# Attention's output projection as four pairs of column tiles by seven block products

## The chip, the core and the metric

The kernel runs on one core of one Trainium2 chip. The metric is the device time of one execution in microseconds (us); three runs gave 1574.85, 1574.91 and 1575.28, median 1574.91.

## What is computed

One inference step of a one-layer streaming encoder, width 1024, on 512 prompt frames and 64 sample frames (576 columns in all, held transposed: features on partitions, frames as columns), in float32:

```python
h = layer_norm(ALPHA * x + 0.5 * swiglu_ffn(x, w_gu, w_down))
z = h @ w_in        # mLSTM q, k, v, o, i, f | attention q, k, v | gates g_ml, g_att
o = band_attention(qa, ka, va)
y_att = o.reshape(b, t, ATT_WIDTH) @ p['w_att_proj']
merged = jax.nn.sigmoid(g_ml) * y_ml + jax.nn.sigmoid(g_att) * y_att
h = layer_norm(ALPHA * h + merged @ p['w_out'])
y = layer_norm(ALPHA * h + 0.5 * swiglu_ffn(h, w_gu2, w_down2))
```

The change is in `y_att`, a product of 1024 by 1024 weights and 1024 by 576 attention outputs, which is then multiplied by the sigmoid of the attention gates.

## The kernel before, in words

**Products.** Every float32 operand is kept as a hi part (rounded, `fp32r`) and a lo part (the rest). A product is three matmuls: hi by hi, hi by lo, lo by hi (`mm3`, and the loops in `gemm` and `product`); `wh`, `wl` are the parts of weights, `os` those of the attention output, `H` those of the layer's input. A column tile is 128 output features; its weights are 1024 columns of SBUF (eight blocks of 128 by 128).

**Plain stages.** `gemm` takes column tiles one after the other, each in two halves of the frames (256 and 320 columns), 24 matmuls a half. Weights come in the order of the list `plan`: `pump` loads a tile on the SP queue into `wr` (two buffers), ScalarE makes the hi part, and for tiles in `ADDED` the lo part comes from ScalarE (minus the hi part) and a second, adding load that GpSimd issues (`add_lo`); other tiles' lo parts are made by VectorE. Four pairs of `wh`, `wl` are there (`NWB`). `pump` converts no tile past the index `wst["stop"]`, which comes from the list `stops`.

**Units by seven products.** In both feed-forwards and in part of the input projection, two column tiles by the two halves of the frames (288 columns each) are made as a unit: with the weights in four blocks and the input in four blocks, seven products of sums of blocks take the place of eight (class `Units`; `Columns` for the input projection). A product is four 128-row blocks by three matmuls, 12 matmuls of 288 columns, and a unit is 84. `Combos.add` makes the sums of the input's blocks, `prep` those of the weights and their parts (`a`: the raw blocks `a12`, `a11`; `s`: sums; `t`, `u`, `b`: parts of sums and of `a22`), by ScalarE (hi) and VectorE (lo, sums). `run` writes out the order: `a11` by `b11`, `a12` by `b21`, in the first unit also the next one's `a11`; then `s2` by `t2`, `s1` by `t1`, `s3` by `t3`, and, after the next unit's first product, `a22` by `t4` and `s4` by `b22`.

**The stage around the change.** After attention's eight pairs of heads, six column tiles of attention's gates (columns 64 to 69 of `w_in`) are plain `gemm`s; gates 6 and 7 were made earlier and lie in DRAM (`GD`). Inside the fourth of them (`j == 3`) attention's pools are closed and the background job `os_split` starts: it splits the eight tiles of attention output (`OT`) into `os` and applies the sigmoid to the first four gates. Background jobs and `later` calls are written into the program while matmuls are counted (`od.tick`). The projection follows: eight plain tiles `("ap", j)`, all in `ADDED`; `ap_cb` multiplies the gate tile by each half on VectorE and stores it to DRAM (`MD`). Behind it starts the mLSTM, with column tiles 8, 9, 0, 1 of `w_in` and their convolution.

TensorE's order is as written; on the other engines and the DMA queues a scheduler orders the instructions by the program and priorities.

Of the kernel before, what the change touches and what calls it, by code (L numbers as in the profile page):

```python
# [10 lines left out]
F32 = mybir.dt.float32  # L11
F32R = mybir.dt.float32r
# [5 lines left out]
P = 128  # L18
# [63 lines left out]
def tile_layer(ctx: ExitStack, tc: tile.TileContext, ins, outs):  # L82
# [30 lines left out]
    def away(s):  # L113

        return dram.tile([P, T], F32, name=nm(s))
# [25 lines left out]
    def act(out, in_, func=AF.Copy, **kw):  # L141
        return ACT.activation(out, in_, func, **kw)  # L142

    def tt(out, a, b, op, eng=None):
        return (eng or DVE).tensor_tensor(out, a, b, op=op)  # L145
# [12 lines left out]
    def blank(out, like, behind=None):  # L158
# [229 lines left out]
    def one(key):  # L388
        return [[(key, KT)]]
# [587 lines left out]
    class Columns(Units):  # L977
# [19 lines left out]

        def done(self, u):
            self.sinks[u["j"]](u["o"])

    class Hidden(Act):

# [620 lines left out]

        act(hs(sg[j], hf), ps, AF.Copy if j <= 3 else AF.Sigmoid)

    for j in range(KT):
        s = slot(F32)
        sg.append(s)
        if j > 5:
            SP.dma_start(s, GD[j])  # L1630
            continue
        gemm(one(("in", 64 + j)), H, [lambda hf, ps, j=j: keep_cb(hf, ps, j)])
        if j == 3:
            od.drain()
            astack.close()
            od.force(lambda: gdone)
            tstack.close()
            ospool = tc.tile_pool(name="os", bufs=16, reuse_waits="tile")
            osp = ostack.enter_context(ospool)
            OS = Act()  # L1640

            osq = []

            def os_split():
                for o_ in OT:
                    hi, lo = slot(F32R, osp, "os"), slot(F32R, osp, "os")
                    act(hi, o_)
                    tt(lo, o_, f(hi), ALU.subtract)
                    yield None
                    OS.p.append((hi, lo))  # L1650
# [7 lines left out]
    MD = [away("md") for _ in range(KT)]  # L1658

    def ap_cb(j):  # L1660
        def cb(hf, ps):
            m = hs(sg[j], hf)
            tt(m, m, ps, ALU.mult)
            if hf == 1:
                SP.dma_start(MD[j], sg[j])
                sg[j] = None
        return cb

    for j in range(KT):
        gemm(one(("ap", j)), OS, [ap_cb(j)])  # L1670
    ostack.close()


# [452 lines left out]
```

## Time and profile before

| what | value |
|---|---|
| runs | 1574.85, 1574.91, 1575.28 us (median 1574.91) |
| profiled execution, its span | 1571.7 us (its own run time is not given apart; the median of the runs lies 3.2 above) |
| TensorE, VectorE, ScalarE, GpSimd busy | 1548.6, 1082.4, 895.5, 214.4 us |
| the projection on TensorE | 801.12 to 852.31 us, no idle time |
| gate tiles 4 and 5 ahead of it | about 788.4 to 801.1 us |
| granted TensorE clock there | 1.00 |

In the rows PE is TensorE, PEld its weight load (beside PE), DVE VectorE, ACT ScalarE, POOL GpSimd, SP the queue that issues most DMAs. A timeline row gives start, length, engine, line, operation, out<-in, shape and count; brackets give the idle time ahead of it and who ended it. L128 is the matmul helper, L142 ScalarE's, L145 and L148 VectorE's two-input helpers, so tiles tell more than lines. Lengths of operations that follow each other on an engine overlap a little.

### The profile page before, as it was taken

To read this page: it belongs to the slowest core of one execution; us is meant where nothing else is said; L and a number is where in the kernel's file an instruction comes from. 1 tells how busy PE (TensorE), PEld (TensorE's weight loads), DVE (VectorE), ACT (ScalarE), POOL (GpSimd) and SP (SyncE) were. 2 spreads that over 40 slices of the span, in tenths; PEclk is the share of its full clock that TensorE was granted. 3 is DMA by queue.
4 is the path that set the end of the run, shared out by engine and by line. 5 is a ranking of instruction groups with operands and counts; after the bars stand their busy time and mean duration, and the time that the engine had idled before them with its cause. 6 is when DMAs were issued, how large, how long until landed. Compare 5 with 4: busy or idle time off the path is not lost.

```text
span 1571.7 us, 29592 instructions
## 1 busy us (share of the span) xinstructions
PE 1548.6 (99%) x11695; PEld 1533.3 (98%) x11695; DVE 1082.4 (69%) x2122; ACT 895.5 (57%) x1668; POOL 214.4 (14%) x403
## 2 busy tenths in 40 slices
PE   9999999999999999999999999999999999999998
PEld 9999999999999999999999999999999999999897
DVE  7777778656898676667522666755786877788546
ACT  7444457423866587777743878653456454557223
POOL 2000001000300143433112222202111000001000
PEclk9999999999999999999999999999999999999999
DMA  9332324434753465665498655552655323225344
GB/s 271 109 108 82 108 81 110 114 114 138 219 157 133 144 163 151 151 160 151 108 261 223 160 135 123 131 152 84 199 146 128 108 81 108 83 88 129 101 125 148
DMA packets 79748, 215.49 MB, mean 137 GB/s; under 512 B 8824, under 2 KB 20728, under 8 KB 79608
## 3 DMA queue, kind: packets, MB, share of 16 engines
q1 hardware_dynamic: 63192, 166.39, 31.5%
q0 software_dynamic: 14688, 44.31, 16.2%
q10 hardware_dynamic: 1728, 2.88, 0.6%
q8 instruction: 92, 1.51, 0.4%
q14 instruction: 48, 0.39, 0.1%
HBM read 181.90 MB, written 19.86 MB: 128 GB/s over the span
## 4 chain that ended last, share of the span: by engine, by line
PE 86%; DVE 6%; ACT 4%; DMA 2%; issue 2%; POOL 0%; SPq 0%; DVEq 0%; ACTq 0%; POOLq 0%
PE mm L128 70%; PE aux L128 14%; PE aux L138 2%; DVE s L148 1%; DVE s L145 1%; DMA w<-in_w_gu 1%; DVE sc L1439 1%; ACT L142 1%; DVE U L148 0%; ACT sc L142 0%; DVE wl L145 0%; ACT s L142 0%; DMA s<-h 0%; ACT wh L142 0%; DMA wr<-in_w_in 0%
## 5 line engine op out<-in xcount | busy, mean ns | idle before, releaser
L128 PE MATMUL mm<-s,wh 128*128 128x288 f32 (+2 forms) x3661 | 748.9, 298 | 8.7 <-DVE s L145 7.0
L128 PEld LDWEIGHTS mm<-s,wh 128*128 128x128 f32 x3661 | 587.8, 189 | 12.4 <-ACT wh L142 4.8
L128 PE MATMUL mm<-s,wl 128*128 128x288 f32 (+2 forms) x1806 | 534.0, 296 | 0.2 <-DVE wl L145 0.2
L128 PEld LDWEIGHTS mm<-s,wl 128*128 128x128 f32 x1806 | 340.8, 189 | 0.4 <-DVE wl L145 0.4
L142 ACT ACTIVATE wh<-wr 128x1024 fp32r<-128x1024 f32 (+2 forms) x144 | 143.3, 996 | 214.8 <-PE mm L128 155.1
L145 DVE TENSOR_TENSOR wl<-wr,wh 128x1024 fp32r<-128x1024 f32 (+2 forms) x86 | 97.3, 1132 | 54.8 <-ACT wh L142 54.7
L128 PE MATMUL mm<-tx,wh 128*128 128x288 f32 x563 | 116.7, 296 | 0.2 <-ACT st L142 0.2
L145 DVE TENSOR_TENSOR wl<-wt,wh 128x1024 fp32r<-128x1024 f32 x48 | 58.8, 1224 | 52.8 <-ACT wh L841 52.8
L841 ACT ACTIVATE wh<-wt 128x1024 fp32r<-128x1024 f32 x48 | 50.8, 1059 | 77.7 <-DVE wt L145 77.5
L128 PEld LDWEIGHTS mm<-tx,wh 128*128 128x128 f32 x563 | 90.7, 188 | 0.5 <-ACT st L142 0.4
L128 PE MATMUL mm<-tx,wl 128*128 128x288 f32 x290 | 85.5, 295 | 0.0
L128 PE MATMUL mm<-h,wh 128*128 128x256 f32 (+2 forms) x384 | 78.4, 295 | 0.0
L190 POOL DMA_DIRECT2D s<-s x16 | 13.7, 854 | 468.3 <-DVE hb L145 424.5
L128 PE MATMUL mm<-tx,ah 128*128 128x288 f32 x360 | 74.0, 297 | 0.6 <-ACT st L142 0.6
L145 DVE TENSOR_TENSOR wl<-wu,wh 128x1024 fp32r<-128x1024 f32 x48 | 58.7, 1223 | 21.7 <-ACT wh L841 21.7
L841 ACT ACTIVATE wh<-wu 128x1024 fp32r<-128x1024 f32 x48 | 50.8, 1058 | 32.7 <-PE mm L128 32.2
L142 ACT ACTIVATE h<-h 128x288 f32<-128x288 f32 x78 | 34.0, 436 | 59.9 <-DVE h L145 59.8
L145 DVE TENSOR_TENSOR s<-s,mm 128x288 f32<-128x288 f32 (+2 forms) x48 | 21.7, 453 | 66.3 <-PE mm L128 66.1
L145 DVE TENSOR_TENSOR wl<-ws,wh 128x1024 fp32r<-128x1024 f32 x48 | 58.6, 1220 | 5.2 <-ACT wh L841 5.2
L128 PEld LDWEIGHTS mm<-h,wh 128*128 128x128 f32 x384 | 61.5, 188 | 0.2
L142 ACT ACTIVATE wl<-wh 128x1024 fp32r<-128x1024 f32 x57 | 60.2, 1056 | 0.4
L128 PEld LDWEIGHTS mm<-tx,ah 128*128 128x128 f32 x360 | 57.3, 188 | 1.4 <-ACT st L142 0.8
(363 smaller groups left out, 3613.9 us busy)
## 6 DMA issues: line engine op xcount, KB each, us to landing
wu<-in_w_gu SPq DMA_DIRECT2D x78, 512.0 KB, 4.4
wr<-in_w_in SPq DMA_DIRECT2D x54, 512.0 KB, 4.0
wl<-in_w_in POOLq DMA_DIRECT2D x46, 512.0 KB, 5.8
wr<-in_w_dn SPq DMA_DIRECT2D x40, 512.0 KB, 3.5
wu<-in_w_in SPq DMA_DIRECT2D x18, 512.0 KB, 4.9
wr<-in_w_dn SPq DMA_DIRECT2D x20, 384.0 KB, 3.4
s<-s POOLq DMA_DIRECT2D x16, 288.0 KB, 4.4
wr<-in_w_ap SPq DMA_DIRECT2D x8, 512.0 KB, 4.9
```

The lines of the kernel that those rows point to most:

```text
L128: PE.matmul(out, lhsT, rhs, start=start, stop=stop, **kw)
L138: PE.transpose(out, in_, idn)
L142: return ACT.activation(out, in_, func, **kw)
L145: return (eng or DVE).tensor_tensor(out, a, b, op=op)
L148: return DVE.scalar_tensor_tensor(out=out, in0=a, scalar=s, in1=b, op0=op0, op1=op1)
L190: return POOL.dma_start(lo, src, accum_op=ALU.add)
L841: self.last = ACT.activation(hi, src, AF.Copy)
L1439: DVE.tensor_tensor_reduce(out=out, in0=ps, in1=g, op0=ALU.add, op1=ALU.max, scale=1.0, scalar=-3e38, accum_out=acc)
```

## The change

The projection becomes a subclass of `Columns`, `Projection`: four units of two column tiles. Its weights leave `plan` and `ADDED` and are loaded into `wu` (two buffers of two tiles) by `Units.load`, their lo parts made by VectorE, and the sums of weight blocks are written over the raw blocks (one 512-column tile `ws` beside them). `os_split` now makes halves `oh` of the last four `OT` tiles, whole parts `os` of the first four, the column sums (in place in the `OT` tiles and in free slots) and their parts `tx`. The gates are multiplied over whole tiles when a unit is complete. Loads of gates 6 and 7 are issued on ScalarE's queue. A new stop in `stops` holds back the conversion of the mLSTM's weights until the last unit.

```diff
     ADDED = {("in", c + j) for c in (32, 40, 48) for j in range(2, KT)} | {("in", c) for c in (*range(32), *range(56, 72))} \
-        | {("ap", j) for j in range(KT)} | {("gu2", 1, 1), ("gu2", 2, 0), ("gu2", 2, 1)}
+        | {("gu2", 1, 1), ("gu2", 2, 0), ("gu2", 2, 1)}
...
-    plan += [(("ap", j), ins["w_ap"][j]) for j in range(KT)]
+    stops.append(len(plan))
...
+    class Projection(Columns):
+        def __init__(self, w, sink, out, wp, combos):
+            Units.__init__(self, [(w[j], w[j + 1]) for j in range(0, KT, 2)], 0, wp, wp, combos)
+            self.sinks, self.out = [lambda o, j=j: sink(j, o) for j in range(0, KT, 2)], out
...
+            w, p = self.raw[j], self.p.setdefault(j, {})
+            a12, a11, a22, a21 = (w[:, i:i + 512] for i in range(0, 2048, 512))
+            if what == "a":
+                p["a12"], p["a11"] = self.parts(w[:, 0:1024])
+            elif what == "s":
+                q = self.ws[j] = self.wp.tile([P, 512], F32, tag="ws", name=nm("ws"), bufs=1)
+                tt(q, a22, a21, ALU.add)
+                tt(a21, a11, a21, ALU.add)
+                tt(a11, q, a11, ALU.add)
+                tt(a12, a11, a12, ALU.add)
+            elif what == "t":
+                p["s4"], p["s2"] = self.parts(w[:, 0:1024])
+            elif what == "u":
+                (p["s1"],) = self.parts(self.ws.pop(j), True)
+            else:
+                p["a22"], p["s3"] = self.parts(w[:, 1024:2048])
+                del self.raw[j]
...
-    for j in range(KT):
+    MD = [away("md") for _ in range(KT)]
+    for j in range(6):
...
-            ospool = tc.tile_pool(name="os", bufs=16, reuse_waits="tile")
+            osp = ostack.enter_context(tc.tile_pool(name="os", bufs=8, reuse_waits="tile"))
             OS = Act()
+            combos = Combos(OS, OT, [x for i in range(4) for x in (None, OT[4 + i])], 16)
...
+            def ap_sink(j, tiles):
+                for e, o in enumerate(tiles):
+                    tt(sg[j + e], sg[j + e], o, ALU.mult)
+                    SP.dma_start(MD[j + e], sg[j + e])
+                    sg[j + e] = None
...
+            un = Projection(ins["w_ap"], ap_sink, opool[0], osp, combos)
+            un.load(0)
+            un.load(1)
...
+                for i in range(4):
+                    hi, lo = (osp.tile([P, HT_], F32R, tag="oh", name=nm("oh")) for _ in range(2))
+                    act(hi, OT[4 + i][:, a])
+                    tt(lo, OT[4 + i][:, a], f(hi), ALU.subtract)
...
+                yield un.prep(0, "a")
...
+                for i in range(4):
+                    combos.sums[2 * i] = slot(F32)
+                    combos.add(i)
+                    halves(i, 1)
+                    yield None
+                    halves(i, 0)
+                    yield None
+                    if i == 1:
+                        yield un.prep(0, "s")
+                    if i == 2:
+                        yield un.prep(0, "t")
...
-            od.bg.append((1300, os_split()))
+            od.bg.append((900, os_split()))
     od.force(lambda: osq)
...
-    for j in range(KT):
-        gemm(one(("ap", j)), OS, [ap_cb(j)])
+    for j in (6, 7):
+        sg.append(slot(F32))
+        ACT.dma_start(sg[j], GD[j])
+    un.load(2)
...
+    def tail():
+        stops.pop(0)
+        wst["stop"] = stops[0]
+        pump(2)
+
+    un.run(tail)
```

On TensorE everything ahead of the projection and behind it stands in the same order; the projection's 384 matmuls become 336. Before, at its start (tile, its weights, the columns):

```order
L128 MATMUL mm_9997<-s_4576,wl_9820 128x320
L128 MATMUL mm_10047<-os_9891,wh_9884 128x256
L128 MATMUL mm_10047<-os_9892,wh_9884 128x256
L128 MATMUL mm_10047<-os_9891,wl_9885 128x256
L128 MATMUL mm_10047<-os_9907,wh_9884 128x256
L128 MATMUL mm_10047<-os_9908,wh_9884 128x256
```

With the change, from the third product (the next unit's `a11`, into `aux`) to the fifth (`s1` by `t1`, weights `ah`); `tx_10088` and `tx_10089` are hi and lo of the last sum `t2`:

```order
L128 MATMUL aux_10149<-oh_9910,wh_10137 128x288
L128 MATMUL aux_10149<-oh_9911,wh_10137 128x288
L128 MATMUL aux_10149<-oh_9910,wl_10138 128x288
L128 MATMUL mm_10107<-tx_9998,wh_10079 128x288
L128 MATMUL mm_10107<-tx_9999,wh_10079 128x288
L128 MATMUL mm_10107<-tx_9998,wl_10080 128x288
...
L128 MATMUL mm_10107<-tx_10088,wh_10079 128x288
L128 MATMUL mm_10107<-tx_10089,wh_10079 128x288
L128 MATMUL mm_10107<-tx_10088,wl_10080 128x288
L128 MATMUL mm_10187<-tx_10011,ah_10141 128x288
```

TensorE now reads, within its first five products, the halves, the whole parts and all sums of the attention output.

On VectorE, between the last tile of attention (`o`) and the first eviction of the projection, stood before only the eight lo parts:

```order
L145 TENSOR_TENSOR o_9433<-aux_9792,tmp_9801 64x512
L145 TENSOR_TENSOR os_9892<-o_6376,os_9891 128x576
L145 TENSOR_TENSOR os_9908<-o_6823,os_9907 128x576
...
L145 TENSOR_TENSOR os_10018<-o_9433,os_10017 128x576
L145 TENSOR_TENSOR s_9434<-s_9434,mm_10047 128x256
```

With the change 42 operations stand from there to the lo part of the last sum `t1` (`tx_10093`); the last twelve of them:

```order
L145 TENSOR_TENSOR tx_10045<-s_10026,tx_10044 128x576
L145 TENSOR_TENSOR s_10083<-o_9433 128x288
L145 TENSOR_TENSOR s_10083<-o_7701,o_9433 128x288
L148 SCALAR_TENSOR_TENSOR o_9433<-s_10083,o_7701 128x288
L145 TENSOR_TENSOR tx_10072<-o_9000,tx_10071 128x576
L148 SCALAR_TENSOR_TENSOR o_9433<-o_9433,o_7701 128x288
L145 TENSOR_TENSOR tx_10076<-s_10066,tx_10075 128x576
L145 TENSOR_TENSOR o_10108<-mm_10123,o_10108 128x288
L145 TENSOR_TENSOR tx_10089<-o_9433,tx_10088 128x576
L145 TENSOR_TENSOR wl_10146<-wu_9887,wh_10145 128x1024
L145 TENSOR_TENSOR tx_10093<-s_10083,tx_10092 128x576
L145 TENSOR_TENSOR ws_10165<-wu_9890 128x512
```

The first eviction of the projection (`o_10108`) now stands among the sums, and the sums of the second unit's weights begin right behind.

At the end of the projection ScalarE with the change makes the parts of the mLSTM's first tiles (`wh_10497` to `wl_10638`) among the copies of the last unit (`o`); the lo parts go on to GpSimd's adding loads:

```order
L142 ACTIVATE o_10328<-mm_10326 128x288
L142 ACTIVATE wh_10497<-wr_9691 128x1024
L142 ACTIVATE wl_10498<-wh_10497 128x1024
L142 ACTIVATE o_10448<-mm_10447 128x288
L142 ACTIVATE o_10449<-mm_10447 128x288
L142 ACTIVATE wh_10504<-wr_9832 128x1024
L142 ACTIVATE wl_10505<-wh_10504 128x1024
L142 ACTIVATE o_10449<-mm_10447 128x288
L142 ACTIVATE wh_10637<-wr_10502 128x1024
```

Before, these tiles followed the projection's own in an even row, two tiles ahead of TensorE; now the second waits for a buffer that the last unit frees two products before its end.

More of the change, by code (lines that the diff above doesn't have):

```diff
@@ L999, in done, with outputs, prep @@
             self.sinks[u["j"]](u["o"])
+    class Projection(Columns):
+        def __init__(self, w, sink, out, wp, combos):
+            Units.__init__(self, [(w[j], w[j + 1]) for j in range(0, KT, 2)], 0, wp, wp, combos)
+            self.sinks, self.out = [lambda o, j=j: sink(j, o) for j in range(0, KT, 2)], out
+        def outputs(self, u):
+            u["o"] = [slot(F32, self.out, "o") for _ in range(2)]
+            for e, o in enumerate(u["o"]):
+                u[f"{e + 1}1"], u[f"{e + 1}2"] = o[:, :HT_], o[:, HT_:]
+        @hot(30)
+        def prep(self, j, what):
+            if j >= self.end:
+                return
+            w, p = self.raw[j], self.p.setdefault(j, {})
[15 more added lines that the diff above has]
+                del self.raw[j]
+            return getattr(self, "last", None)
     class Hidden(Act):
@@ L1637, in tile_layer @@
             tstack.close()
-            ospool = tc.tile_pool(name="os", bufs=16, reuse_waits="tile")
-            osp = ostack.enter_context(ospool)
+            osp = ostack.enter_context(tc.tile_pool(name="os", bufs=8, reuse_waits="tile"))
             OS = Act()
+            combos = Combos(OS, OT, [x for i in range(4) for x in (None, OT[4 + i])], 16)
+            combos.pool = osp
             osq = []
-            def os_split():
-                for o_ in OT:
+            def ap_sink(j, tiles):
[3 more added lines that the diff above has]
+                    sg[j + e] = None
@@ new lines, in tile_layer @@
+            un = Projection(ins["w_ap"], ap_sink, opool[0], osp, combos)
+            un.load(0)
+            un.load(1)
+            def os_split():
+                a, b = slice(0, HT_), slice(HT_, T)
+                OS.p = [None] * KT
+                for i in range(4):
+                    hi, lo = (osp.tile([P, HT_], F32R, tag="oh", name=nm("oh")) for _ in range(2))
+                    act(hi, OT[4 + i][:, a])
+                    tt(lo, OT[4 + i][:, a], f(hi), ALU.subtract)
+                    OS.p[4 + i] = hi, lo
+                yield None
+                yield un.prep(0, "a")
+                for i in range(4):
@@ L1646, in os_split, with halves @@
                     hi, lo = slot(F32R, osp, "os"), slot(F32R, osp, "os")
-                    act(hi, o_)
-                    tt(lo, o_, f(hi), ALU.subtract)
+                    act(hi, OT[i])
+                    tt(lo, OT[i], f(hi), ALU.subtract)
+                    OS.p[i] = hi, lo
                     yield None
-                    OS.p.append((hi, lo))
+                def halves(i, n):
+                    t, hi, lo = combos.sums[2 * i + n], combos.tile(), combos.tile()
+                    act(hi, t)
+                    tt(lo, t, f(hi), ALU.subtract)
+                    d = combos.b.setdefault(i, {})
+                    for k, c in zip(("t2", "t4") if n else ("t1", "t3"), (a, b)):
+                        d[k] = hi[:, c], lo[:, c]
@@ new lines, in os_split @@
+                for i in range(4):
+                    combos.sums[2 * i] = slot(F32)
[3 more added lines that the diff above has]
+                    halves(i, 0)
+                    yield None
+                    if i == 1:
+                        yield un.prep(0, "s")
+                    if i == 2:
+                        yield un.prep(0, "t")
+                for i in range(4):
+                    (h1, l1), (h2, l2) = OS.p[4 + i], OS.p[i]
+                    combos.b[i].update(b11=(h1, l1), b21=(h2[:, a], l2[:, a]), b22=(h2[:, b], l2[:, b]))
@@ L1654, in os_split @@
                 yield None
-            od.bg.append((1300, os_split()))
+            od.bg.append((900, os_split()))
     od.force(lambda: osq)
[L1658 to L1667, printed above, removed]
-    for j in range(KT):
-        gemm(one(("ap", j)), OS, [ap_cb(j)])
+    for j in (6, 7):
[7 more added lines that the diff above has]
+    un.run(tail)
     ostack.close()
```

3 lines of the change are left out of this document (removed).

## The prediction

> **What bounds the kernel now.** I read the page first: busy times, then the chain that ended last.
>
> ```profile
> span 1571.7 us, 29592 instructions
> PE 1548.6 (99%) x11695; PEld 1533.3 (98%) x11695; DVE 1082.4 (69%) x2122; ACT 895.5 (57%) x1668; POOL 214.4 (14%) x403
> PE 86%; DVE 6%; ACT 4%; DMA 2%; issue 2%; POOL 0%; SPq 0%; DVEq 0%; ACTq 0%; POOLq 0%
> ```
>
> TensorE is busy for 99% of the span and holds 86% of the chain. A change pays here by taking columns off TensorE, provided that nothing else is then late. Next come the view by stretches (times, then busy us and records of PE, PEld, DVE, ACT, POOL, granted clock, DMA share, GB/s), TensorE's timeline at the two edges of the projection, and the tile view of its inputs `os`.
>
> ```profile
> 782.00:801.20 19.20, 19.20 (x146) 19.20 (x145) 5.83 (x9) 13.66 (x23) 2.53 (x3) 1.00 0.77 205
> 801.20:852.30 51.10, 51.10 (x385) 51.10 (x384) 6.80 (x15) 17.13 (x17) 7.30 (x10) 1.00 0.92 246
> 801.12 0.40 PE L128 MATMUL mm<-os,wh 128*128 128x256 f32 x2
> 852.31 0.40 PE L128 MATMUL mm<-s,wh 128*128 128x256 f32 x2
> L128 PE MATMUL mm<-os,wl x128: 283/296/309, 801.4 to 852.2; 128*128 128x256 f32 x64, 128*128 128x320 f32 x64
> ```
>
> The projection runs from 801.12 to 852.31, 51.19 us for 384 matmuls (128 with a lo weight, and twice as many with a hi one), and TensorE never waits in it, nor in the 19 us ahead. VectorE is busy 6.8 of 51.1 us, and 5.8 of 19.2 ahead: there is room for its new work.
>
> **The columns saved.** Four pairs by seven products by 12 matmuls are 336 matmuls, all of 288 columns, for 384 that average 288. The same class of unit already runs ahead of attention. Two VectorE evictions of neighbouring units there, both released by TensorE, give its period; a stretch of the first feed-forward gives a second rate.
>
> ```profile
> 510.00 0.46 DVE L145 TENSOR_TENSOR st<-mm,st 128x288 f32<-128x288 f32 x1 [0.37 <-PE mm L128]
> 521.19 0.46 DVE L145 TENSOR_TENSOR st<-mm,st 128x288 f32<-128x288 f32 x1 [0.32 <-PE mm L128]
> 60.00:280.00 220.00, 220.00 (x1659) 219.79 (x1658) 177.53 (x253) 120.61 (x199) 6.50 (x8) 1.00 0.31 100
> ```
>
> A unit of 84 matmuls takes 11.19 us, so four take 44.76 and a product takes 1.60. That saves 51.19 - 44.76 = **6.43 us**. By the second rate (220.00 / 1659 = 132.6 ns) it is 6.6; I take 6.43, from the like unit, and keep 6.6 as the end.
>
> **What is removed beside it** gives nothing: 16 ScalarE operations on weights, eight adding loads of GpSimd and 16 evictions of VectorE lay beside a TensorE that had no idle time. The loads of stored gates 6 and 7 go from the SP queue to ScalarE's; eight loads of `og` and two of `vf` move behind the projection on SP. Their first readers come late, and four issues on ScalarE's queue took 1.88 us:
>
> ```profile
> L138 PE MATMUL aux<-ident,vf x20: 271/272/274, 873.5 to 917.1; 128*128 128x128 f32 x16, 128*64 128x128 f32 x4
> L148 DVE SCALAR_TENSOR_TENSOR og<-aux,cols,og x4: 275/510/747, 923.9 to 929.1; 128x512 f32<-128x512 f32 x2, 128x64 f32<-128x64 f32 x2
> 0.81 1.88 ACTq L454 DMA_DIRECT2D s<-in_xT  x4
> ```
>
> `vf` is read 21 us behind the projection's end, `og` 71: cost 0. The two issues of 0.47 us wait on ScalarE for VectorE's lo parts; only the last hi part of the sums stands behind the first of them, and VectorE splits it three operations later anyway: 0, unless VectorE is late. On SP the weights of pairs three and four wait for VectorE's last reading of the first two; behind them stand stores that nobody awaits in the stage and weight loads of the next stage, due a unit later: 0.
>
> **What is added ahead of the first unit.** This is the disputed term. Before TensorE can finish product five (`s1` by `t1`), VectorE must have done 42 operations in one row: four lo halves, four whole lo parts, four 512-column weight sums, 16 operations of the column sums, four lo parts of weights of 1024, one of 512, eight lo parts of the sums, one eviction. Their durations and distances (group rows: busy, mean ns; timeline rows: start, length):
>
> ```profile
> 419.76 0.45 DVE L148 SCALAR_TENSOR_TENSOR st<-st,s 128x288 f32<-128x288 f32 x1
> 420.13 0.46 DVE L145 TENSOR_TENSOR st<-s 128x288 f32<-128x288 f32 x1
> 504.06 0.69 DVE L145 TENSOR_TENSOR wt<-ws,wu 128x512 f32<-128x512 f32 x1
> 504.78 0.69 DVE L145 TENSOR_TENSOR wt<-wt,wu 128x512 f32<-128x512 f32 x1
> 506.62 1.23 DVE L145 TENSOR_TENSOR wl<-wt,wh 128x1024 fp32r<-128x1024 f32 x1 [0.49 <-ACT wh L841]
> 507.76 1.22 DVE L145 TENSOR_TENSOR wl<-ws,wh 128x1024 fp32r<-128x1024 f32 x1
> 786.46 3.44 DVE L145 TENSOR_TENSOR os<-o,os 128x576 fp32r<-128x576 f32 x5 [0.66 <-ACT os L142]
> L145 DVE TENSOR_TENSOR os<-o,os x8: 752/756/759, 785.0 to 792.4; 128x576 fp32r<-128x576 f32 x8
> ```
>
> Starts lie 0.37 us apart at 288 columns, (3.44 - 0.76) / 4 = 0.67 at 576, 1.14 at 1024, 0.72 for a 512 that reads the one before (I take 0.62 for a free one: 0.69 less the 0.07 to 0.09 by which the others overlap). The row is 21 x 0.37 + 12 x 0.67 + 4 x 1.14 + 4 x 0.72 + 0.62 = 23.9 us; by full lengths it is 21 x 0.46 + 12 x 0.76 + 4 x 1.23 + 5 x 0.69 = 27.2. When it can begin, and when the weights arrive:
>
> ```profile
> 779.47 1.25 PE aux L128 x7
> 780.81 0.59 ACT L142 ACTIVATE tmp<-aux 64x512 f32<-64x512 f32 x1 [1.79 <-PE aux L128]
> 781.97 1.06 ACT L142 ACTIVATE wh<-wr 128x1024 fp32r<-128x1024 f32 x1 [0.57 <-PE mm L128]
> wu<-in_w_in SPq DMA_DIRECT2D x6, 512.0 KB, 4.6
> wr<-in_w_ap SPq DMA_DIRECT2D x3, 512.0 KB, 7.7
> ```
>
> ScalarE's next work behind `tmp` is now an eviction that TensorE releases at 781.97, then the first hi half: VectorE starts about 782.8, and without a pause ends at 806.7. Product five reads the last lo in its eleventh matmul, 801.12 + 4 x 1.60 + 10 x 0.133 = 808.85. So 2.2 us are left for pauses. The load of the first pair of weights overwrites memory that the last matmuls of attention read, until 780.72; it lands 4.6 us later (785.3) in the quiet case, 7.7 us later (788.4) at the projection's load of before. ScalarE reaches it about 786, so the quiet case costs nothing, and the traffic of before (0.77 to 0.92 of DMA) loses its adding loads. Where the like units begin, VectorE was as full:
>
> ```profile
> 467.00:478.00 11.00, 11.00 (x85) 11.00 (x84) 10.96 (x18) 6.65 (x11) 0.00 (x0) 1.00 0.32 101
> 478.00:489.00 11.00, 10.19 (x75) 9.73 (x74) 9.51 (x14) 9.06 (x15) 0.00 (x0) 1.00 0.44 159
> 480.14 0.53 PE L128 MATMUL mm<-tx,wh 128*128 128x288 f32 x2 [0.20 <-ACT st L142]
> 484.18 0.53 PE L128 MATMUL mm<-tx,ah 128*128 128x288 f32 x2 [0.61 <-ACT st L142]
> ```
>
> TensorE lost 0.2 + 0.6 = 0.8 us there. So the added stall lies between 0 and, by full lengths with 1 us of pauses (the two waits and a little), 782.8 + 27.2 + 1.0 - 808.85 = 2.1 us. A gain is excluded, since TensorE had no idle time here. I take **0.4**, half of that nearest row. In the later units VectorE has 3 x 1.14 + 0.62 + 4 x 0.72 + 3 x 0.37 + 2 x 0.67 = 9.4 us of 11.19, against 177.53 x 11.19 / 220 = 9.0 in the feed-forward, where TensorE never waited: 0.
>
> On VectorE the Trainium skill, "VectorE: DVE Perf Modes", section "The DRAIN you can't avoid", speaks against this change: the next operation does not start until the pipeline of the one before is empty, and leaving out waits doesn't help. Taken as full lengths it would give the first rival's time; the starts 0.37 apart of operations 0.45 long say that it does not hold to the full length here.
>
> **What is added at the end.** The weights of the next stage used to be split 19, 13 and 6 us ahead; now conversion stops at the last gate tile and starts again inside the last unit. The first tile's buffer is freed six products before the end E, the second's two products before it.
>
> ```profile
> 839.57 1.06 ACT L142 ACTIVATE wh<-wr 128x1024 fp32r<-128x1024 f32 x1 [4.25 <-PE mm L128]
> 842.01 0.86 POOL L190 DMA_DIRECT2D wl<-in_w_in  x1 [5.55 <-ACT wl L142]
> DMA to landing us min/median/max: 5.2/6.0/9.0
> ```
>
> The third row is the landing of the adding loads between 757 and 880. From the hi part to the adding load are 842.01 - 839.57 = 2.44 us, and 6.0 to its landing. First tile: E - 9.6 + 2.4 + 6.0 = E - 1.2, read at E + 0.2. Second: E - 3.2 + 2.4 + 6.0 = E + 5.2, read a tile of 6.40 later, at E + 6.6. Both have 1.4 us to spare; at the slowest landing, 9.0, both come 1.6 late, but one delay covers the other. Bounds 0 and 1.6; I take **0**, by the median.
>
> **Sum.** -6.43 + 0.4 + 0 = -6.0 us on the profiled span of 1571.7. The runs' median, 1574.91, lies 3.2 above that span; I leave that distance alone: 1574.91 - 6.0 = **1568.9**.
>
> **The rivals.**
> - *VectorE is late at product five* (full lengths, or weights landing at 788.4 instead of 785.3): a stall of about 2.1, -6.43 + 2.1 = -4.3, 1570.6. For it: the row is 42 operations long and alternates with ScalarE. Against: 2.2 us of slack, and 10.96 of 11 us busy in the like row.
> - *The adding loads are late at the end*: -6.43 + 0.4 + 1.6 = -4.4, 1570.5. For it: stores and loads crowd there; against: the median landing.
> - *Slower: every unit is bound by VectorE.* The sums in place form a chain (each waits for the last, the lo parts follow, only then may the next weights be loaded). The change breaks even at 51.19 / 4 = 12.80 us a unit, 1.61 more than 11.19; at 10.1 us of VectorE by full lengths plus 3.4 of waits, 13.5 a unit, it gives +2.8, 1577.7, and beyond 14.2 a unit it is slower by over 0.2%. Against: 1.8 us free in each unit.
> - *It does not do what it says*: were TensorE's row the same, the time would be. The order shows 48 matmuls fewer and the rest in place, so I give it next to nothing.
>
> **How the numbers follow.** Forecast 0.69, VectorE late 0.16, end late 0.08, several of these together so that less than 0.2% is gained 0.04, bound units 0.03. The low end is no stall at the quicker rate, 1574.91 - 6.6 = 1568.3, less 0.2 for the runs' spread; the high end takes in both single late cases and a third of the way from there to their sum (1572.2): 1571.2. 0.2% (3.1 us) is about what a measurement of this kernel tells from no change: faster 0.92, same 0.05, slower 0.03.
>
> **What the profile after would show.** 336 matmuls from about 801.1 to 846.3, with `tx`, `oh` and `os` as inputs; TensorE idle time, if any, at the fourth to sixth product (805.9 to 810) or 0 to 8 us behind the end; VectorE some 85% busy in the stretch, GpSimd with no adding load of the projection. Wrong would be: a unit longer than 11.3 us, idle time of TensorE above 1 us in the stretch, or a next stage that loses more than it did.

## The result, and the profile after

The change makes the kernel slower. Twenty runs of it have a median of 1580.03 us (1576.91 to 1588.07), twenty of the kernel before 1575.37 (1573.08 to 1581.00); the ratio is 1.0028, 95% interval 1.0015 to 1.0040. Forecast were 1568.9 us, 1568.1 to 1571.2, with a chance of 0.03 for slower.

The profiled execution is one of the longest (1587.94 us). First its page: span, busy times, chain.

```profile
span 1586.2 us, 29561 instructions
PE 1552.2 (98%) x11647; PEld 1535.6 (97%) x11647; DVE 1123.1 (71%) x2182; ACT 904.4 (57%) x1692; POOL 208.3 (13%) x395
PE 83%; DVE 6%; DMA 4%; ACT 4%; issue 2%; POOL 0%; SPq 0%; DVEq 0%; ACTq 0%; POOLq 0%
```

DMA has doubled its share of the chain, from 2% to 4%. Next the projection, by stretches (columns as before: busy us and records of PE, PEld, DVE, ACT, POOL, granted clock, DMA share, GB/s): the four units one by one, then all of it.

```profile
810.24:821.43 11.19, 11.19 (x87) 11.19 (x86) 10.41 (x19) 7.02 (x13) 0.00 (x0) 1.00 0.45 146
821.43:832.60 11.17, 11.17 (x86) 11.17 (x85) 10.34 (x14) 5.21 (x8) 0.00 (x0) 1.00 0.42 150
832.60:843.80 11.20, 11.20 (x87) 11.20 (x86) 9.24 (x14) 5.28 (x9) 0.00 (x0) 1.00 0.15 55
843.80:854.77 10.97, 10.97 (x84) 10.97 (x84) 4.48 (x7) 7.23 (x10) 1.52 (x2) 1.00 0.64 159
810.24:854.77 44.53, 44.53 (x338) 44.53 (x337) 34.48 (x52) 24.73 (x38) 1.52 (x2) 1.00 0.41 127
```

The projection itself does what was forecast, and better: 44.53 us for 51.19, no wait of TensorE, 6.66 us saved. Its DMA share falls from 0.92 to 0.41. The loss lies behind it. TensorE's timeline there has three long waits (L138 is the helper of the transposes); of before the same stretch had one, of 0.23 us.

```profile
863.16 0.39 PE L128 MATMUL mm<-s,wl 128*128 128x256 f32 x1 [1.59 <-DMA wl<-in_w_in]
884.97 1.11 PE L138 MATMUL aux<-ident,qf 128*128 128x128 f32 x4 [3.60 <-ACT qf L142]
888.87 0.42 PE L138 MATMUL aux<-ident,qf 128*64 128x128 f32 x1 [2.79 <-DVE kwl L148]
```

The granted clock (third column from the right) falls to half within the second of these waits (it is 0.97 from 882 to 884) and is half until 894:

```profile
884.00:886.00 2.00, 1.03 (x4) 0.71 (x4) 0.95 (x3) 2.00 (x7) 0.18 (x1) 0.50 1.08 257
890.00:894.00 4.00, 4.00 (x17) 4.00 (x16) 2.27 (x7) 3.09 (x9) 1.54 (x6) 0.50 0.08 13
896.00:898.00 2.00, 2.00 (x19) 2.00 (x18) 1.00 (x3) 2.00 (x6) 0.24 (x1) 1.00 0.51 147
```

**The sum.** The projection starts 9.12 us later than before, at 810.24, though TensorE's order ahead of it is the same: in this execution the clock fell to half there as well, behind waits at 333, 384 and 407 us (0.57 at 334 to 338, 0.50 at 410 to 416; 1.00 in the profile of before). That is the luck of one execution (in the other profiled executions the projection starts at 800.3 to 803.7), so I count from the projection's first matmul to the end of the span: 1571.7 - 801.12 = 770.58 before, 1586.2 - 810.24 = 775.96 after, 5.38 more (by the medians 4.66). It is made of -6.66 for the columns, +7.75 for the waits (1.59 + 3.60 + 2.79 - 0.23), about +2.9 for TensorE's work at half clock (1.1 us of transposes and 4.7 us from 889.3 to 894, half of each), and 1.4 more. Of these some 0.5 go in small steps between the waits up to 894; from there on the two kernels run alike to TensorE's last group of matmuls (1576.88, before 1563.24, so 4.52 later by this count), and the last 0.9 lie behind it, at the very end of the program.

**Who waits for what.** The chain of waits (start, length, what) names two loads: `wr`, the raw weights of a column tile, and `c`, the first head's state of the mLSTM. The timelines of ScalarE and of SP's queue follow them.

```profile
855.33 11.60 DMA wr<-in_w_in
...
868.96 9.93 DMA c<-in_C
```

```profile
867.02 1.06 ACT L142 ACTIVATE wh<-wr 128x1024 fp32r<-128x1024 f32 x1 [7.13 <-DMA wr<-in_w_in]
878.91 0.64 ACT L142 ACTIVATE ch<-c 128x516 fp32r<-128x516 f32 x1 [3.51 <-DMA c<-in_C]
883.51 0.38 ACT L142 ACTIVATE R<-mm 128x256 f32<-128x256 f32 x1 [1.35 <-DVE U L148]
```

```profile
868.10 0.33 SPq L252 DMA_DIRECT2D wr<-in_w_in  x1
868.53 0.38 SPq L1844 DMA_DIRECT2D og<-od  x1
868.96 0.52 SPq L1886 DMA_DIRECT2D c<-in_C  x1
```

Of before, the two instructions on `c` (SP's queue, then ScalarE), and the landing of the loads from 12 us ahead of the projection's end to 16 us behind it:

```profile
854.42 0.45 SPq L1813 DMA_DIRECT2D c<-in_C  x1
```

```profile
861.05 0.64 ACT L142 ACTIVATE ch<-c 128x516 fp32r<-128x516 f32 x1
```

```profile
wr<-in_w_in SPq DMA_DIRECT2D x4, 512.0 KB, 5.0
wl<-in_w_in POOLq DMA_DIRECT2D x4, 512.0 KB, 6.1
vf<-vd SPq DMA_DIRECT2D x2, 288.0 KB, 3.2
```

The same view of after, and its three stretches of 8 us from the projection's end:

```profile
wr<-in_w_in SPq DMA_DIRECT2D x5, 512.0 KB, 6.4
wl<-in_w_in POOLq DMA_DIRECT2D x5, 512.0 KB, 9.0
vf<-vd SPq DMA_DIRECT2D x2, 288.0 KB, 13.4
```

```profile
854.64:862.64 8.00, 6.93 (x53) 6.73 (x51) 1.78 (x6) 3.85 (x5) 6.11 (x18) 1.00 0.97 263
862.64:870.64 8.00, 7.48 (x56) 7.44 (x57) 2.00 (x3) 2.39 (x4) 1.15 (x3) 1.00 1.03 274
870.64:878.64 8.00, 7.99 (x63) 7.75 (x62) 1.63 (x3) 3.54 (x9) 0.54 (x4) 1.00 1.05 344
```

Before, `c` was issued 2.1 us behind the projection's end and was there by 8.7 us behind it, when ScalarE came to it; now it is issued 14.2 us behind and lands after 24.1. The late `wr` has a part in that: ScalarE stands 7.13 us for it, SP's queue issues nothing from 861.3 until ScalarE has read it (868.08), and `c` is two places behind the `wr` that SP issues then. The DMA engines, busy for 0.41 of the projection, have no free time for 24 us behind it (0.97 to 1.05; before, 0.99, 0.72 and 0.69), and by the medians above the loads take longer. ScalarE runs nothing while it stands at `wr` and at `ch`: the evictions `R` and the `qf` of the next column tiles, which TensorE's transposes need, stand behind it.

### The profile page after: what moved, and what is told of

Its sections match the earlier page's. It is cut to its first block, busy times and chain, and to the rows that moved or that the text cites. A ratio compares the mean times of both kernels' runs of the same rounds, so it can differ in the third digit from the quotient of the medians.

```text
span 1586.2 us, 29561 instructions
## 1 busy us (share of the span) xinstructions
PE 1552.2 (98%) x11647; PEld 1535.6 (97%) x11647; DVE 1123.1 (71%) x2182; ACT 904.4 (57%) x1692; POOL 208.3 (13%) x395
## 4 chain that ended last, share of the span: by engine, by line
PE 83%; DVE 6%; DMA 4%; ACT 4%; issue 2%; POOL 0%; SPq 0%; DVEq 0%; ACTq 0%; POOLq 0%
PE mm L128 67%; PE aux L128 14%; PE aux L138 2%; DMA wr<-in_w_in 1%; DVE s L145 1%; DVE s L148 1%; DMA c<-in_C 1%; DVE wl L145 1%; DMA w<-in_w_gu 1%; ACT wh L142 1%; DMA wr<-in_w_dn 1%; DMA s<-in_xT 0%; ACT s L142 0%; DVE U L148 0%; ACT sc L142 0%
## 5 line engine op out<-in xcount | busy, mean ns | idle before, releaser
L142 ACT ACTIVATE wh<-wr 128x1024 fp32r<-128x1024 f32 (+2 forms) x136 | 134.8, 992 | 188.9 <-PE mm L128 119.0
L128 PE MATMUL mm<-tx,wh 128*128 128x288 f32 x635 | 131.3, 296 | 0.2 <-ACT st L142 0.2
L128 PEld LDWEIGHTS mm<-tx,wh 128*128 128x128 f32 x635 | 102.2, 188 | 0.5 <-ACT st L142 0.4
L128 PE MATMUL mm<-tx,wl 128*128 128x288 f32 x326 | 96.1, 295 | 0.0
L145 DVE TENSOR_TENSOR wl<-wu,wh 128x1024 fp32r<-128x1024 f32 x60 | 73.4, 1223 | 26.4 <-ACT wh L841 26.4
L841 ACT ACTIVATE wh<-wu 128x1024 fp32r<-128x1024 f32 x60 | 63.5, 1059 | 36.9 <-PE mm L128 33.6
L128 PE MATMUL mm<-tx,ah 128*128 128x288 f32 x392 | 80.5, 297 | 0.6 <-ACT st L142 0.6
L142 ACT ACTIVATE h<-h 128x288 f32<-128x288 f32 x78 | 34.0, 436 | 59.9 <-DVE h L145 59.8
L190 POOL DMA_DIRECT2D wl<-in_w_in x46 | 39.8, 865 | 176.9 <-ACT wl L142 95.8
L128 PEld LDWEIGHTS mm<-tx,wl 128*128 128x128 f32 x326 | 61.2, 188 | 0.0
```

What stands on the lines that cost most here:

```text
L128: PE.matmul(out, lhsT, rhs, start=start, stop=stop, **kw)
L190: return POOL.dma_start(lo, src, accum_op=ALU.add)
L841: self.last = ACT.activation(hi, src, AF.Copy)
```

## The experiments

Each ratio is against the kernel before, run on the same chip (medians: 1576.89 beside `og_late`, `before_og`, `lo_vec` and `og_c_lo`; 1576.79 beside `c_early`, `ch_late`, `ch_lo` and `warm`; 1576.80 beside `warm2`, `margin` and `c_lo`; 1576.01 beside `warm3` and `c_first`). It is the recorded ratio with its 95% interval; the quotient of the medians can differ from it by up to 0.001.

### og_late, before_og: is it the loads of og?

My first theory (A) was the eight loads of `og`, 2.3 MB, which the change puts behind the projection. One kernel takes them out of there, the other puts them there in the kernel before.

```diff
-            SP.dma_start(st["og"][e], OD[2 * h + e])
...
-            SP.dma_start(outs["pC"][h, :, e, :], cn)
+            stored = SP.dma_start(outs["pC"][h, :, e, :], cn)
+            with tc.issue_after(stored.ins):
+                SP.dma_start(st["og"][e], OD[2 * h + e])
```

> The changed kernel with the eight loads of og issued on SP behind the stores of the mLSTM's first states (two by two, one head at a time) instead of in the first 25 us behind the projection. Theory A (the og loads, pushed behind the projection, fill the DMA engines there, and the next weights and the state c land late): TensorE's idle time behind the projection falls from 8.0 us to under 2, the granted clock stays at 1.00 there, and the time is 1568 to 1571 us. Theory B (the weights of the next stage are simply asked for too late, since conversion stops until the last unit): idle time stays above 5 us and the time above 1575 us. Theory C (both are needed): as A.

Measured: 1582.51 us, ratio 1.0028 (1.0012 to 1.0044), no better than the change. The first wait is gone; the others are longer, and the chain names `c`, which now leaves earlier and is on its way longer:

```profile
851.75 14.18 DMA c<-in_C
```

```profile
870.53 1.67 PE L138 MATMUL aux<-ident,qf 128*128 128x128 f32 x5 [6.01 <-ACT qf L142]
881.60 0.30 PE L138 MATMUL aux<-ident,qf 128*64 128x128 f32 x1 [2.64 <-DVE vl L145]
```

```diff
-                SP.dma_start(MD[j], sg[j])
+                stored[0] = SP.dma_start(MD[j], sg[j])
...
-            SP.dma_start(st["og"][e], OD[2 * h + e])
+            with tc.issue_after(stored[0].ins):
+                SP.dma_start(st["og"][e], OD[2 * h + e])
```

> The kernel before with one thing of the change alone: its eight loads of og, which it issued ahead of and in the projection, stand behind the projection's last store on SP, in the order of the changed kernel. Theory A: the same loads make the same traffic, TensorE idles 3 to 8 us at 865 to 885 us and the time is 4 to 12 us above the kernel before. Theory B: no loss, within 1 us. Theory C (late loads of og hurt only where the weights come just in time): within 2 us of the kernel before, since its weights are two tiles ahead.

Measured: 1577.62 us, ratio 1.0005 (0.9987 to 1.0024). The same loads fill the DMA engines here too (the second and third 8 us behind the projection, and the landing of `c`), and TensorE loses 0.64 us. Here `c` is issued 3.2 us behind the projection, ahead of six of the eight.

```profile
859.46:867.46 8.00, 8.00 (x63) 7.96 (x62) 3.69 (x6) 5.31 (x13) 1.70 (x7) 1.00 1.05 272
867.46:875.46 8.00, 8.00 (x64) 7.99 (x63) 4.59 (x8) 6.53 (x14) 1.43 (x5) 1.00 1.04 324
```

```profile
c<-in_C SPq DMA_DIRECT2D x1, 258.0 KB, 6.8
```

Theory A falls on both sides. Full DMA engines alone cost nothing that these runs can tell; the next ones ask whether it matters that a load for which an engine stands waiting is among the late ones.

### lo_vec: fewer loads

```diff
-        | {("gu2", 1, 1), ("gu2", 2, 0), ("gu2", 2, 1)}
+        - {("in", c) for c in (0, 1, 8, 9)} | {("gu2", 1, 1), ("gu2", 2, 0), ("gu2", 2, 1)}
```

> The changed kernel with the lo parts of the mLSTM's first four column tiles (8, 9, 0, 1) made by VectorE and not by GpSimd's adding loads; the loads of og stay where the change put them. Theory B (weights asked for too late, the adding load being the last link): all three waits of TensorE behind the projection go, 1568 to 1571 us. Theory A: the first wait (1.59 us on the adding load) goes, those behind it (3.60 and 2.79 us) stay for the most part, since c and the loads of weights still share the DMA engines with og: 1574 to 1578 us.

Measured: 1573.81 us, ratio 0.9976 (0.9960 to 0.9991). Four adding loads of 512 KB are gone, and with them four operations of ScalarE (`wl`, 1.06 us each); `c` is issued 9.1 us behind the projection's end and lands 8.75 us later, and one wait is left, with the clock at 1.00 behind it:

```profile
872.71 0.30 PE L138 MATMUL aux<-ident,qf 128*64 128x128 f32 x1 [2.87 <-DVE kwl L148]
```

```profile
868.74:884.74 16.00, 13.13 (x102) 12.89 (x101) 11.41 (x24) 15.43 (x36) 5.05 (x15) 1.00 0.48 112
```

So this edit takes away a large part of the loss, but not all; the result lies between the two theories. It doesn't separate the traffic of the adding loads from ScalarE's work on them.

### og_c_lo: everything eased

> The changed kernel with both edits (og late, lo parts of tiles 8, 9, 0, 1 by VectorE) and the first head's state c loaded into a free slot inside the last unit. All theories: no wait of TensorE behind the projection above 0.5 us, and the columns saved come through whole: 51.2 - 44.5 = 6.7 us less than the kernel before, about 1568.3 us; if it stays above 1571 us, a cause is missing.

Measured: 1570.95 us, ratio 0.9959 (0.9945 to 0.9973), 5.9 us less than the kernel before by the medians and 6.5 by the ratio; no wait behind the projection until 909 us. The columns do come through, so nothing else of the change costs more than some tenths of a microsecond.

### c_early, ch_late, ch_lo: is it c?

`c_early` loads `c` inside the last unit; `ch_late` leaves it late, but makes its parts where they are needed.

```diff
     def tail():
...
+        c00.append(slot(F32)[:, 0:516])
+        SP.dma_start(c00[0].rearrange("p (e c) -> p e c", c=258), ins["C0"][0])
...
-        c0 = mp.tile([P, 516], F32, tag="c0", name=nm("c0"))
+        c0 = mp.tile([P, 516], F32, tag="c0", name=nm("c0")) if h else c00[0]
```

> The changed kernel with one thing different: the first head's state c is loaded into a free slot inside the last unit, instead of behind the projection, behind the next weights on SP. After the og runs Theory A is down: og late left c 14.2 us on the way and TensorE idle for 6.0 and 2.6 us. Theory D: c's landing (24 us behind the projection's end in the changed kernel) holds up ScalarE, which works in order and has c's hi part ahead of the evictions and of qf: the waits of 3.60 and 2.79 us and the half clock behind them go, the first wait (1.59 us, adding load) may stay; 1569 to 1573 us. Theory E (all loads behind the projection are late, c is only one of them): another load ends the waits in its place, above 1575 us.

Measured: 1571.68 us, ratio 0.9961 (0.9946 to 0.9975). The waits are 0.31 and 0.79 us, and no half clock stands behind them.

```profile
861.51 0.38 PE L128 MATMUL mm<-s,wl 128*128 128x256 f32 x1 [0.31 <-DMA wl<-in_w_in]
873.99 0.30 PE L138 MATMUL aux<-ident,qf 128*64 128x128 f32 x1 [0.79 <-DVE vl L145]
```

```diff
-        act(ch, c0v)
-        tt(cl, c0v, f(ch), ALU.subtract)
         st["C"] = (c0v, ch, cl)
...
-            act(qs_[:, 0], qt)
-            tt(qs_[:, 1], qt, f(qs_[:, 0]), ALU.subtract)
+            a = act(qs_[:, 0], qt)
+            b = tt(qs_[:, 1], qt, f(qs_[:, 0]), ALU.subtract)
+            c0v, ch, cl = st["C"]
+            with tc.issue_after(a.ins):
+                act(ch, c0v)
+            with tc.issue_after(b.ins):
+                tt(cl, c0v, f(ch), ALU.subtract)
```

> The changed kernel with c loaded as late as there, but its hi and lo part made some 25 us later on ScalarE and VectorE, behind the parts of qsc, so that neither engine stands waiting for it. Theory D: as c_early, 1569 to 1573 us. Theory E: above 1575 us, with a wait on weights (wr, wl) or on vf in place of c.

Measured: 1571.79 us, ratio 0.9971 (0.9956 to 0.9985); waits of 0.53 us on an adding load and 1.53 us on `vl`. The edit moves no load, only the place at which ScalarE and VectorE come to `c` (which is issued 11.0 us behind the projection's end).

> ch_late together with the lo parts of the column tiles 8, 9, 0, 1 by VectorE; the loads of og and c stay where the change put them. Theory D: both links of the loss are gone, no wait above 0.6 us behind the projection, 1568 to 1570.5 us. Theory E: waits of 2 us and more stay.

Measured: 1569.96 us, ratio 0.9957 (0.9940 to 0.9974), 6.8 us less than the kernel before. The DMA engines are less full in the first 8 us behind the projection (0.76 for 0.97), then nearly as full as with the change, and TensorE does not wait:

```profile
847.00:855.00 8.00, 8.00 (x64) 8.00 (x63) 4.26 (x9) 2.97 (x6) 4.59 (x15) 1.00 0.76 271
855.00:863.00 8.00, 8.00 (x63) 7.96 (x62) 4.09 (x6) 5.55 (x12) 1.47 (x6) 1.00 0.93 278
863.00:871.00 8.00, 8.00 (x64) 7.99 (x63) 4.97 (x11) 6.54 (x17) 1.63 (x6) 1.00 1.05 333
```

Theory D holds: without ScalarE's stop at `c`, taken away in two ways, the loss of 0.28% becomes a gain of 0.3 to 0.4%. That the adding loads are a second link shows in `lo_vec` and in the traces, where the waits that `c_early` and `ch_late` keep are gone here; in time these three kernels lie within each other's intervals.

### c_lo: og once more

> The changed kernel with c loaded early into a free slot, as in c_early, and the lo parts of the column tiles 8, 9, 0, 1 by VectorE; the loads of og stay where the change put them, so that it is og_c_lo without its first edit. If og's place costs nothing once c and the adding loads are out of its way: the same as og_c_lo and ch_lo, 1569 to 1571 us beside a kernel before of 1576.8. If og still costs something: 2 us and more above them, with a wait on a load.

Measured: 1569.72 us, ratio 0.9956 (0.9944 to 0.9968). With `c` early and four adding loads gone, the place of `og` costs nothing that shows (0.9956 against 0.9959 for `og_c_lo`). This and `ch_lo` are the best kernels of the study; both beat the kernel before by what the columns promise.

### c_first: does the place on SP's queue suffice?

```diff
-        SP.dma_start(c0v, ins["C0"][h])
+        with tc.high_priority(offset=0 if h else 600):
+            SP.dma_start(c0v, ins["C0"][h])
```

> The changed kernel with c loaded into the same tile as there, but issued on SP ahead of the last store, the two next weights, vf and og, as soon as its memory is free. If c is late because of what stands ahead of it on SP and on the way (the bunched weights, stores and og): it lands by 12 us behind the projection's end, ScalarE does not wait for it, and the time is 1569 to 1573 us as with c_early. If its memory comes free so late that the queue behind it is held up: a wait for weights in its place, above 1575 us.

Measured: 1577.26 us, ratio 1.0011 (0.9995 to 1.0027), between `c_early` and the change. `c` leaves at 847.92 and ScalarE's `ch` starts at 855.3, 8 us behind the projection's end instead of 24, but ScalarE still stood waiting for it, by 3.2 us; five waits of 0.53 to 2.37 us stay, on `wl`, `qf`, `kwl` and `vl`. The place on the queue was part of its lateness; behind it the others are late in its place: ScalarE now waits 5.3 us for two loads of `wr`. The time is that of the second case expected, though not for its reason, since the memory of `c` came free early.

This run makes sense by the time for which ScalarE stands for loads within 40 us behind the projection's end, beside TensorE's waits there (us; one profiled execution each):

| kernel | ScalarE for `wr` | for `c` | TensorE's waits |
|---|---|---|---|
| before | 0 | 0 | 0.2 |
| `before_og` | 0 | 1.1 | 0.6 |
| `c_lo`, `og_c_lo` | 2.5 | 0 | 0 |
| `ch_lo` | 3.0 | 0 | 0 |
| `c_early` | 4.0 | 0 | 1.1 |
| `ch_late` | 5.2 | 0 | 2.1 |
| `lo_vec` | 5.5 | 2.8 | 2.9 |
| `c_first` | 5.3 | 3.2 | 5.3 |
| the change | 8.5 | 3.5 | 8.0 |
| `og_late` | 4.5 | 9.4 | 8.7 |

By and large TensorE's waits go with the two columns together, and not with `c` alone. In `warm`, `warm2` and `warm3`, which are the changed kernel with added matmuls, ScalarE's two stops add up to 11.2 to 11.4 us, of which `c` has 4.1 to 6.8: the sum hardly changes from one execution to the next, its division does. No run takes away the stops at `wr` and leaves that at `c`.

### margin: how near was VectorE?

Four operations of 1024 columns more in the row ahead of the first unit, on top of `ch_lo`.

```diff
                     if i == 2:
+                        for _ in range(4):
+                            tt(spare, spare, spare, ALU.add)
                         yield un.prep(0, "t")
```

> ch_lo with four more VectorE operations of 1024 columns (on a tile that nothing else reads) in the row ahead of the first unit's fifth product; the row ended 0.9 us ahead of its reader in the changed kernel. If VectorE's row is what the first unit would wait for, as the prediction's first rival has it, TensorE now stalls for 4 x 1.14 to 4 x 1.24 less 0.9, that is 3.7 to 4.1 us, in the first unit, and the time is 3 to 5 us above ch_lo. If the row has more room than it seems, below 2 us.

Measured: 1576.57 us, 6.6 above `ch_lo`; its projection lasts 51.39 us instead of 44.53. TensorE's waits are 2.93 + 0.68 = 3.6 us, nearly as expected, and the half clock (0.50) that comes with them takes some 3 more, which the expectation of 3 to 5 had not counted.

```profile
812.05 0.61 PE L128 MATMUL mm<-tx,wh 128*128 128x288 f32 x1 [2.93 <-ACT tx L142]
813.33 0.61 PE L128 MATMUL mm<-tx,wh 128*128 128x288 f32 x1 [0.68 <-DVE tx L145]
```

```profile
812.00:818.00 6.00, 5.27 (x20) 4.96 (x21) 4.38 (x6) 2.67 (x4) 0.00 (x0) 0.50 0.30 91
```

### warm, warm2, warm3: is the half clock the waits' own?

Matmuls without use fill TensorE's idle time, in the changed kernel (the edit of `warm3`):

```diff
+            if len(turns) == 3:
+                for _ in range(32):
+                    PE.matmul(latest["mm"][:, 320:512], H.p[0][0][:, :P], H.p[0][0][:, :192], start=True, stop=True,
+                              skip_group_check=True)
             ps = bank()
```

> The changed kernel with 30 matmuls of 256 columns, whose results are overwritten, ahead of the first transposes of qf, that is where TensorE stands idle for 3.60 us. They take about 30 x 0.11 = 3.3 us, nearly all of it time in which TensorE waits anyway. If the half clock behind the wait comes from TensorE having been idle, it stays at 1.00 there or falls for less, and from the first matmul of the projection to the end the span is 3 to 5 us shorter than the changed kernel's 775.96 us. If the clock falls for another reason (load, time), it falls as before, and the span is the same or up to 1 us longer.

> The changed kernel with twice 24 matmuls of 256 columns (results overwritten or never read) at the place where the first try had missed it: ahead of the two parts of the second turn of qf, where TensorE idles for 3.60 and 2.79 us in the changed kernel. 24 x 0.11 = 2.6 us each, nearly all of it time in which TensorE waits anyway. If the half clock comes from TensorE's idleness, it stays at 1.00 from 875 to 895 us, and from the first matmul of the projection to the end the span is 3 to 5 us shorter than the changed kernel's 775.96 us, so about 771 to 773. If it falls for another reason: the same 776, or up to 2 us more.

Neither answers the question: in `warm` (1585.18 us, ratio 1.0048, 1.0030 to 1.0065) the matmuls stood one turn too early and the waits of 4.11 and 2.86 us came behind them; in `warm2` (1585.73, 1.0058, 1.0046 to 1.0070) they waited for VectorE themselves, 9.15 us, since the tile that they wrote was still being read.

> The changed kernel with twice 32 matmuls of 192 columns ahead of the two parts of the second turn of qf, now into columns 320 to 511 of the bank that TensorE is filling itself, so that they wait for no engine (the first try stood at another place, the second waited for VectorE). 32 x 0.08 = 2.6 us each, in the 3.60 and 2.79 us in which TensorE idles there. If the half clock comes from TensorE's idleness, it stays at 1.00 from 875 to 900 us, and from the first matmul of the projection to the end the span is 3 to 5 us shorter than the changed kernel's 775.96 us, 771 to 773. If it falls for another reason: 776 to 778 and the same half clock.

In `warm3` they start without a wait (and spoil some sums of column tile 1, in whose bank they write). It takes 1582.99 us, ratio 1.0050 (1.0031 to 1.0068): they last 7.5 us instead of 5.2, and a new wait comes behind. But the clock of this execution answers: it is at 1.00 where the old waits are filled, and half behind the new one. (In this kernel the helpers stand four lines lower, so that L142 is the transposes and L146 ScalarE's.)

```profile
871.97 3.72 PE L1822 MATMUL mm<-s 128*128 128x192 f32 x32
877.04 0.66 PE L142 MATMUL aux<-ident,qf 128*128 128x128 f32 x4 [1.36 <-ACT qf L146]
877.46 3.80 PE L1822 MATMUL mm<-s 128*128 128x192 f32 x32
...
892.90 0.39 PE L132 MATMUL aux<-vh,kwh 128*128 128x258 f32 x1 [2.85 <-ACT vh L146]
```

```profile
872.00:888.00 16.00, 14.64 (x123) 14.47 (x123) 9.62 (x19) 14.58 (x30) 5.00 (x14) 1.00 0.53 153
892.00:896.00 4.00, 2.75 (x12) 2.55 (x13) 3.53 (x6) 1.95 (x5) 1.15 (x3) 0.67 0.95 241
```

Here the half clock goes with TensorE's waits. This is one execution, and `lo_vec` had a wait of 2.87 us without it; what all the traces show of it stands in the last section. Its price without the waits was not had: the expected 3 to 5 us of gain did not come.

## Why the prediction was wrong, step by step

- **The columns saved**: right in kind and slightly low. 6.66 us against 6.43: 336 matmuls at 132.5 ns, as the second rate (6.6) had it.
- **VectorE's row ahead of the first unit**: no stall instead of 0.4. Its 42 operations ran from 792.11 to 816.98, 24.9 us, where the sum by start distances said 23.9 and by full lengths 27.2. So the rule of the Trainium skill that spoke against the change ("VectorE: DVE Perf Modes", section "The DRAIN you can't avoid"), taken as full lengths, does not hold here. The last lo part was done at 816.98; its reader, the second matmul of the last block, came at 817.76 + 0.13 = 817.89. 0.9 us were left of the 2.2 that I had, and `margin` shows what lay behind them.

```profile
816.23 0.75 DVE L145 TENSOR_TENSOR tx<-s,tx 128x576 fp32r<-128x576 f32 x1
```

```profile
817.76 0.43 PE L128 MATMUL mm<-tx,ah 128*128 128x288 f32 x2
```

- **Later units**: right, no wait, with VectorE busy up to 10.3 of 11.17 us.
- **The adding loads at the end**: the mechanism was right and its size wrong. I took the median landing of 6.0 us, and none late; the slowest landing, 9.0, was the median after the change, and the first wait was 1.59 us, the bound of 1.6 almost to the digit.
- **What is moved costs nothing**: this is the step that failed. I asked of each moved load when its own reader comes (`vf` 21 us behind, `og` 71), and found all in time. I did not ask whom they and the bunched weights delay, nor where `c` would stand, which the change does not touch: its load fell from 2.1 to 14.2 us behind the projection's end, and its reader stands on ScalarE ahead of work that TensorE needs. Where I wrote of SP "weight loads of the next stage, due a unit later: 0", those loads came late themselves (11.6 us on the way for one `wr`) and held `c` back. The sum gave this step 0; in the profile TensorE's waits behind the projection grew by 7.75 us (1.59 of it on the adding load), while ScalarE stood 8.5 us for `wr` and 3.5 for `c`. Take away the stop at `c` (`c_early`, `ch_late`) and most of the loss goes; with the adding loads alone taken away (`lo_vec`) a good part does; with both (`ch_lo`, `c_lo`) TensorE waits no more. `og`, the largest of the moved loads, was not a link by itself.
- **No term for the clock**: every wait was priced at its length. With TensorE's waits at the seam came half clock, some 2.9 us on top of 7.75.

The rivals had the right place (the end) and too small a price; the one on the slower side, units bound by VectorE, was another mechanism. (Its "14.2 a unit" is also a slip: by its own numbers 0.2%, 3.1 us, is passed at 12.8 + 3.1 / 4 = 13.6.) Of the signs of being wrong the last one came, a next stage that loses more than it did. That the pressure goes from the DMA share of the projection to that of the next stage was in the order of the loads on SP and not weighed.

## What to carry to other kernels

When a stage gets shorter or stops loading for the next one, add up the bytes that must now land in the first microseconds of the next stage, and find the loads whose reader stands early on an engine that works in order: the delayed load need not be one that the change moved. Load such small state early, or make its parts only where they are read; with four adding loads less, either turned 0.28% slower into 0.43 to 0.44% faster here. A wait of TensorE costs more than its length when half clock follows it.

## What the runs showed of the hardware

- **Half clock behind short waits.** Around the waits of 3.60 and 2.79 us the granted clock was 0.50 for some 10 us. The Trainium skill ("TensorE: Matmul & The Clock Gate", section "Part 1: The HAM clock gate (the "warmup" mystery)") says that about 3.4 us without work bring the half clock. The longest waits here agree in part: half clock came with all four above 3.4 us (3.60 with the change, 4.11 in `warm`, 6.01 in `og_late`, 9.15 in `warm2`), but with the change it began 2.5 us into the wait and in `og_late` 2.3. And with the change a wait of 1.82 us was followed by 0.57, while one of 1.74 us at the same place of the kernel before was followed by 1.00, and the 2.87 us of `lo_vec` too: no length at which it decides shows in these runs, and it differs from one execution to the next. The place at 333 us has a wait of 1.74 to 2.01 us in all fifteen profiled executions; half clock followed in six. Every stretch of half clock ahead of TensorE's last matmuls is 3.4, 6.8 or 10.2 us long, and each begins within a wait of 1.44 us or more or at most 2.3 us behind one.

```profile
333.13 0.50 PE L128 MATMUL mm<-s,wh 128*128 128x288 f32 x2 [1.82 <-DVE s L145]
```

```profile
334.00:338.00 4.00, 4.00 (x21) 4.00 (x20) 2.72 (x7) 0.00 (x0) 0.00 (x0) 0.57 0.55 165
```

- **Narrow matmuls.** The two rows of 32 matmuls of 192 columns took 3.72 and 3.80 us, the last one's own 0.28 included, so they start 111 and 114 ns apart, where I had expected 80; 256 columns take 120 in the stage behind the projection (0.36 us for three). A quarter fewer columns saved 5 to 8%.
- **One load, 6.8 to 14.2 us.** The same 258 KB of `c` took 6.8 us in `before_og` and 14.18 in `og_late`, both with the DMA engines full (a share of 0.98 and 1.01 in that time).
